# A two-layer encoder kernel on one Trainium2 core: 96 idle bytes at each end of the SBUF pools

## The chip, the cores and the metric

The kernel runs on one core of a Trainium2 chip. A core has TensorE (PE, with its weight loads shown as PEld), VectorE (DVE), ScalarE (ACT), GpSimd (POOL) and SyncE (SP, which here issues every DMA). Operands lie in SBUF, a memory of 128 partitions, and matrix products land in PSUM. The metric is the device time of one execution, in microseconds; lower is better. The figure of a kernel is the median of its runs.

## The reference

The reference is a two-layer encoder on one sequence of 1024 tokens with 1024 features, all in float32. Cut to what matters:

```
for i in range(2):
    shift, scale, gate = split(silu(c) @ ada_w[i] + ada_b[i], 3)
    h = rmsnorm(x, norm_g[i]) * (1 + scale) + shift
    y = diff_attention(h, ...) if i == 0 else latent_attention(h, ...)
    x = x + gate * y
return rmsnorm(x, final_norm_g)
```

Layer 0 is differential attention: 8 heads, two softmaxes of width 64 for each head, the second one subtracted with a learned factor, then a norm for each head, a SiLU gate, and an output projection. Layer 1 is latent attention: queries, keys and values come out of two narrow projections (384 and 256 wide), 64 of the query and key features are rotated by position, 8 heads of width 128, a SiLU gate, an output projection.

## The kernel before, in words

Features or tokens lie on the 128 partitions, and a matrix product is tiled in 128x128 weights times up to 512 moving columns. To reach float32 accuracy every operand is held as two float32r tiles, a high part and a low part, and a product is three matmuls into one PSUM bank (`mm3`, lines 176 to 180):

```
PE.matmul(psum, ah, bh, start=first, stop=False)
PE.matmul(psum, ah, bl, start=False, stop=False)
PE.matmul(psum, al, bh, start=False, stop=last)
```

The first operand is the one loaded as weights, the second one streams. In the names of the profile, `oacc<-woh,o1b3h` is a matmul into `oacc` that streams `woh` over the weights `o1b3h`.

The order of the work is written out by hand: the layer 0 input projection while the modulation weights come in (up to some 180 us), attention of layer 0 with the rest of its projections filled in between the heads (to 676 us), output projection 0, the input projections of layer 1 (lines 1192 to 1514), attention of layer 1, and output projection 1 (`out_proj`, line 1016). Attention lets the PE do, for each block of 128 queries, the scores (L767 in layer 0, L1605 in layer 1), four transposes at a time of the exponentials (L376, streaming the constant tile `ident`), and the products with V (L178 to L180, 256 columns). Fills are steps of a stream of projections (`Stream`, `gen_strips`). SP issues all DMAs in program order.

SBUF is handed out by two stacks of pools. A pool opened with `side="left"` (the default, line 88) lies above the ones that are open on the left; one with `side="right"` lies below those that are open on the right. The two stacks grow toward each other, and a pool that opens where another one has closed waits, tile by tile, for the old tiles' users. On the left lie, from below, `const` (line 98: `ident`, `ones`, `cosT`, `sinT` and small vectors) and `sm` (line 99: small tiles of a few values); above them come and go `p1a`, `a0a`, `pm`, `a0b` (layer 0), `kpp`, `h1`, `p3x`, `p3`, `p4`, `p4v` (projections), `attn1`, `attn1b`, `p6`. On the right the outermost is `wst` (line 126, the weight strips `wraw`, `wh`, `wl`), and below it `H`, `wp0`, `p1b`, `xp`, `OT0`, `pw0`, `u`, `wp1`, `lora`, `pv1`, `OT1`, `pw1`.

A tile takes a multiple of 32 bytes in each partition. The large tiles have 1024, 2048 or 4096 bytes, so all large tiles of one side share their remainder to 128. In the program as built, the first large tile of `const` starts at byte 16512, a multiple of 128. The small tiles of `const` and `sm` then shift what lies above: the lowest large tile of the left pools starts at byte 28064, which is 32 more than a multiple of 128 (and 160 more than a multiple of 256). The right stack ends at byte 229344, and its large tiles, such as `wraw` at byte 206816, lie 96 above a multiple of 128 (224 above a multiple of 256). Between the two stacks at least 576 bytes are free at every time.

A product's two operands can therefore lie on the same side or on opposite ones. Counted over the program's matmuls by the addresses of their two operands: 3849 matmuls of 512 columns have both on one side (2856 right, 993 left); 627 of 512 columns have them on opposite sides (513 stream a left tile over right weights, 114 the reverse), and 18 of 256 columns do. The 1566 products with V of 256 columns are all left with left. 1152 transposes stream `ident`. Of the 627, 300 are in the layer 1 input projections (the first four token blocks of `h1` and the combination tiles `t4` lie on the left, the strips in `wst` on the right), 327 in the two output projections, where `p3` and `p6` hold their late weights on the left and `OT0`, `xp`, `OT1` the attention outputs on the right, or where the pools are the other way round.

Of the kernel before, what the change touches and what calls it, by code (L numbers as in the profile page):

```python
# [11 lines left out]
F32 = mybir.dt.float32  # L12
# [9 lines left out]
P = 128  # L22
# [46 lines left out]
X_CUT = 256  # L69
FIN_LAG = 1  # L70
SKEW = 1
GUARD = 2.0 ** 40
FMAX = 3.4028e38
LAM0 = 0.8 - 0.6 * math.exp(-0.3 * 0)
# [9 lines left out]
def trunk(ctx: ExitStack, tc: tile.TileContext, A, out):  # L84
# [3 lines left out]
    def pool(stack, name, bufs=1, side="left", space=None):  # L88
        kw = dict(name=name, bufs=bufs, reuse_waits="tile")
        if space is not None:  # L90
            kw["space"] = space
            if space == DRAM:
                kw.pop("reuse_waits")
        else:
            kw["side"] = side
        return stack.enter_context(tc.tile_pool(**kw))

    const = pool(ctx, "const")
    sm = pool(ctx, "sm", bufs=4)
    pst = ExitStack()  # L100
    ps = None
    NB = {}
# [20 lines left out]
        return ps.tile(shape or [P, HF], F32, name=name, tag=tag, bufs=NB[tag])  # L123

    dr = pool(ctx, "dr", bufs=1, space=DRAM)
    wst = pool(ctx, "wst", side="right")


# [17 lines left out]
    def part(name):  # L146
        lo, n = VEC[name]
        return vec[:, lo : lo + n]
# [6 lines left out]
    g8 = const.tile([P, 1], F32, name="g8")  # L155
    V.tensor_scalar(g8, part("subln_g"), 0.5 * (1.0 - LAM0) * math.sqrt(P) / GUARD, None, op0=ALU.mult)
    qag, kvg, inv = part("q_a_norm_g"), part("kv_a_norm_g"), part("inv")
# [136 lines left out]
    side = Side()  # L294
# [152 lines left out]
    def gen_mods(load, c2):  # L447

        g, bsh, bsc, a_, b_ = mods[1]
        for j in range(KT):  # L450
            for i, (bias, acc) in enumerate(((bsh, b_), (bsc, a_))):
                mod_dot(load(A["ada_ss1"][j, i]), bias[:, j : j + 1], acc[:, j : j + 1], c2)
                if j == KT - 1 and i == 1:
                    V.scalar_tensor_tensor(out=a_, in0=a_, scalar=1.0, in1=g, op0=ALU.add, op1=ALU.mult)
                yield
        yield from gen_gate(0, load, c2)
# [16 lines left out]
    def h_chunk(l, xn4, k, dst, hp, sub=G, wide=False, act=False, f32=None):  # L473

        _, _, _, a_, b_ = mods[l]
        if wide:
            tr = bank("cb", "trc", [P, D])[:, :HF].rearrange("p (j q) -> p j q", j=4)
        else:
            tr = bank("tr", "trh", [P, 4, P])
        for j in range(len(xn4)):  # L480
            nk = KT // len(xn4[j])
            PE.transpose(tr[:, j, :], xn4[j][k // nk][:, (k % nk) * P : (k % nk + 1) * P], ident)
        n = len(xn4)
        hh, hl = dst
        ak, bk = a_[:, k : k + 1], b_[:, k : k + 1]
        tmp = f32.rearrange("p (j q) -> p j q", j=4) if f32 is not None else hp.tile([P, n, P], F32, name="h32", tag="h32", bufs=2)
        S.activation(hh, tr[:, :n, :], AF.Identity, bias=bk, scale=ak)
        if act:
            S.activation(tmp, tr[:, :n, :], AF.Identity, bias=bk, scale=ak)
        else:  # L490
            V.tensor_scalar(tmp, tr[:, :n, :], ak, bk, op0=ALU.mult, op1=ALU.add)
        return sub.tensor_sub(hl, tmp, f32v(hh)).ins
# [110 lines left out]
    mods_g = gen_mods(lambda src: mod_home[0](src), c2)  # L603
    for k in range(-1, KT + SKEW):
        if k + 1 < KT:
# [18 lines left out]
        if 0 <= k < KT:  # L624
            h_chunk(0, xs0, k, h0[k][0], p1, act=True)
        if k < SKEW:
            continue
        k0, (wh, wl) = k - SKEW, wv0[k - SKEW]
        hh, hl = h0[k0][0]
# [200 lines left out]
    def head_out(o_, o, sq):  # L830


        S.activation(sq, o_, AF.Square, scale=1.0 / GUARD)
        S.mul(o, o_, g8[:, 0:1])

    def subln(o, sq, zz, half, h, dst):
# [7 lines left out]
        def rest():  # L844
# [5 lines left out]
            V.tensor_mul(fin, zz, zz)  # L850
            V.scalar_tensor_tensor(out=w, in0=fin, scalar=P * EPS / GUARD ** 2, in1=pt[:, 0:4], op0=ALU.mult, op1=ALU.add)
            V.scalar_tensor_tensor(out=fin, in0=fin, scalar=FMAX / GUARD ** 2, in1=w, op0=ALU.mult, op1=ALU.is_ge)
            V.tensor_scalar(w, w, 3.0e38, None, op0=ALU.min)
# [983 lines left out]
```

## Time and profile before

| what | value |
|---|---|
| median of 3 runs | 1440.59 us (1439.78 to 1441.86) |
| span of the profiled execution, first to last instruction | 1437.4 us |
| its time beside the span | not given apart; the median lies 3.2 us above the span |
| mean granted TensorE clock in it | 0.995 of full speed |
| matmuls in it | 7388 |

The page of the profile gives the busy time of each engine, the same in 40 slices of the span, the DMA queues, the chain of work that ended last, and the costliest groups of instructions. Matmuls overlap: a 128x512 matmul shows a duration near 390 ns, while the next one starts some 230 ns after it. So the pace of TensorE is read from starts, not from durations. In a timeline row the columns are start, duration, engine, line, operation, output and inputs, shapes and count.

### The profile page before, as it was taken

The numbers are of one execution on the slowest core, as the hardware profiler recorded it, in microseconds if no ns is written. First come the engines' busy times: TensorE is split into PE (matmuls) and PEld (weight loads), VectorE is DVE, ScalarE is ACT, GpSimd is POOL, SyncE is SP. The second block draws the span as 40 slices with busy tenths as digits, with TensorE's granted clock in tenths as the row PEclk, the third lists the DMA queues.
The fourth block names the chain that finished last, engine by engine and source line by source line (L and its number), as shares of the span: only waits on it lengthen the run. The fifth ranks groups of instructions, "written<-read, shape, count | busy, mean of one in ns | idle before, by whom it ended". The sixth has DMA issues, their size and how long they took to land. (4 is left out here: it accounts for less than half of the span.)

```text
span 1437.4 us, 20644 instructions
## 1 busy us (share of the span) xinstructions
PE 1388.9 (97%) x7388; PEld 1159.2 (81%) x7388; DVE 920.2 (64%) x1372; ACT 727.4 (51%) x1287; POOL 611.7 (43%) x483
## 2 busy tenths in 40 slices
PE   5999999999999999998999999999999999999997
PEld 4778788888888887887777877887888888888886
DVE  6657777667777767677435885545666555555355
ACT  5533366656565656566343443335455554545342
POOL 4416064656464646463562334532141331412572
PEclk9999999999999999999999999999999999999999
DMA  9787823233333333337663146398343433336563
GB/s 329 236 247 224 264 67 103 81 105 83 100 87 97 91 93 89 88 96 237 227 201 124 40 132 190 122 296 246 125 128 114 130 98 78 105 97 212 188 234 140
DMA packets 135527, 213.70 MB, mean 149 GB/s; under 512 B 19072, under 2 KB 56064, under 8 KB 135424
## 3 DMA queue, kind: packets, MB, share of 16 engines
q1 hardware_dynamic: 135424, 212.38, 48.6%
q8 instruction: 58, 0.95, 0.3%
q14 instruction: 45, 0.37, 0.1%
HBM read 137.92 MB, written 50.80 MB: 131 GB/s over the span
## 5 line engine op out<-in xcount | busy, mean ns | idle before, releaser
L378 ACT CAST pth<-tr 128x512 fp32r<-128x512 f32 x256 | 150.2, 587 | 282.4 <-PE tr L376 280.8
L393 DVE TENSOR_REDUCE nm<-s 128x1 f32<-128x1024 f32 x192 | 233.9, 1218 | 75.6 <-PE s L767 64.1
L379 DVE TENSOR_TENSOR ptl<-tr,pth 128x512 fp32r<-128x512 f32 x256 | 176.0, 687 | 139.0 <-ACT pth L378 138.4
L224 POOL TENSOR_TENSOR wl<-wraw,wh 128x512 fp32r<-128x512 f32 (+2 forms) x79 | 104.0, 1319 | 204.5 <-ACT wh L223 196.0
L395 ACT ACTIVATE e<-s,nm 128x1024 f32<-128x1024 f32 x128 | 143.5, 1121 | 29.2 <-DVE nm L393 28.7
L376 PE MATMUL tr<-ident,e 128*128 128x128 f32 x1024 | 154.9, 274 | 2.5 <-DVE ptl L379 2.3
L376 PEld LDWEIGHTS tr<-ident,e 128*128 128x128 f32 x1024 | 121.3, 140 | 43.3 <-DVE ptl L379 19.6
L178 PE MATMUL acc<-h0h,wh 128*128 128x512 f32 x360 | 149.9, 416 | 2.1 <-DVE v_hl L356 2.0
L178 PE MATMUL pv<-pth,vt 128*128 128x256 f32 x512 | 147.2, 288 | 0.2 <-DMA vt<-vS 0.2
L179 PE MATMUL pv<-ptl,vt 128*128 128x256 f32 x512 | 145.9, 285 | 0.0
L180 PE MATMUL pv<-pth,vt 128*128 128x256 f32 x512 | 144.6, 282 | 0.0
L180 PE MATMUL acc<-h0h,wl 128*128 128x512 f32 x360 | 142.3, 395 | 0.5 <-POOL wl L224 0.5
L179 PE MATMUL acc<-h0l,wh 128*128 128x512 f32 x360 | 141.4, 393 | 0.0
L1007 POOL TENSOR_TENSOR wol<-wor,woh 128x512 fp32r<-128x512 f32 x64 | 86.3, 1373 | 83.3 <-ACT woh L1006 78.1
L178 PEld LDWEIGHTS pv<-pth,vt 128*128 128x128 f32 x512 | 97.6, 191 | 3.5 <-DMA vt<-vS 0.7
L179 PEld LDWEIGHTS pv<-ptl,vt 128*128 128x128 f32 x512 | 97.7, 191 | 2.6
L180 PEld LDWEIGHTS pv<-pth,vt 128*128 128x128 f32 x512 | 97.7, 191 | 0.1
L320 POOL TENSOR_TENSOR rp_r<-rp_raw,cosT 128x512 f32<-128x512 f32 x38 | 49.8, 1311 | 92.2 <-ACT rp_raw L315 52.1
L325 POOL TENSOR_TENSOR rp_sw<-rp_sw,sinT 128x512 f32<-128x512 f32 x42 | 54.9, 1307 | 76.1 <-DMA rp_sw<-rp_raw 69.6
L767 PE MATMUL s<-ks,qa 128*128 128x512 f32 x256 | 82.1, 402 | 3.6 <-DVE e L775 3.2
L775 DVE SCALAR_TENSOR_TENSOR e<-s,z,e 128x1024 f32<-128x1024 f32 x64 | 82.1, 1283 | 2.1
L767 PE MATMUL s<-ks,qb 128*128 128x512 f32 x256 | 80.9, 395 | 0.0
(590 smaller groups left out, 3340.3 us busy)
## 6 DMA issues: line engine op xcount, KB each, us to landing
ada<-in_ada_ss SPq DMA_DIRECT2D x32, 512.0 KB, 5.9
wraw<-in_w_s SPq DMA_DIRECT2D x64, 256.0 KB, 3.0
vS<-v_hl SPq DMA_DIRECT2D x32, 512.0 KB, 5.8
vt<-vS SPq DMA_DIRECT2D x32, 512.0 KB, 4.2
wor<-in_w_out SPq DMA_DIRECT2D x64, 256.0 KB, 4.2
rp_sw<-rp_raw SPq DMA_DIRECT2D x168, 64.0 KB, 2.0
bc_s<-bc_d SPq DMA_DIRECT2D x34, 256.0 KB, 4.3
oS<-bc_s SPq DMA_DIRECT2D x30, 256.0 KB, 2.5
```

The costliest lines, as they stand in the source:

```text
L178: PE.matmul(psum, ah, bh, start=first, stop=False)
L179: PE.matmul(psum, ah, bl, start=False, stop=False)
L180: PE.matmul(psum, al, bh, start=False, stop=last)
L224: sub = (V if pair_of else G).tensor_sub(l_[:, :n], raw[:, :n], f32v(h_[:, :n]))
L376: PE.transpose(tr[:, j, :], p[:, kt * P : (kt + 1) * P], ident)
L378: mk["S"] = S.copy(pth[kh][:, :, dst], tr).ins
L379: mk["V"] = V.tensor_sub(ptl[kh][:, :, dst], tr, f32v(pth[kh][:, :, dst])).ins
L393: mk["V"] = V.reduce_max(nm, s_ps, axis=AX.X, negate=True).ins
L395: mk["S"] = S.activation(e, s_ps, AF.Exp, bias=nm, scale=1.0, accum_out=zs).ins
L767: PE.matmul(s_ps[:, kc * HF : (kc + 1) * HF], src[:, c, ql], KS[h][kc][:, c, :], start=fst, stop=not fst)
L775: combined.append(V.scalar_tensor_tensor(out=e0, in0=e1, scalar=z1[:, 0:1], in1=e0, op0=ALU.mult, op1=ALU.add).ins)
L1007: in_turn(G.tensor_sub(lo, raw, f32v(hi)))
```

## The change

Two pools are added, each with one tile that nothing reads or writes. `padl` opens on the left above `const` and `sm` and takes 96 bytes; `padr` opens first on the right and takes 96 bytes at the top. Both stay open to the end. Every later left tile moves up by 96 bytes and every right tile down by 96.

```diff
@@ -69,6 +69,8 @@
 SKEW = 1
+PADL = 96 // 4
+PADR = 96 // 4
 GUARD = 2.0 ** 40
@@ -97,6 +99,8 @@
     const = pool(ctx, "const")
     sm = pool(ctx, "sm", bufs=4)
+    padl = pool(ctx, "padl")
+    padl.tile([P, PADL], F32, name="padl")
     pst = ExitStack()
@@ -123,6 +127,8 @@
     dr = pool(ctx, "dr", bufs=1, space=DRAM)
+    padr = pool(ctx, "padr", side="right")
+    padr.tile([P, PADR], F32, name="padr")
     wst = pool(ctx, "wst", side="right")
```

By the addresses above, the left large tiles then start at 28160, a multiple of 512, and the right ones, as `wraw` at 206720, lie 128 above a multiple of 256. No instruction, DMA, wait or size is added or taken away.

## The prediction

> **What bounds the kernel now.** I read the page first: the busy shares, the slices, the chain that ended last.
>
> ```profile
> span 1437.4 us, 20644 instructions
> ...
> PE 1388.9 (97%) x7388; PEld 1159.2 (81%) x7388; DVE 920.2 (64%) x1372; ACT 727.4 (51%) x1287; POOL 611.7 (43%) x483
> ...
> PE   5999999999999999998999999999999999999997
> ...
> PEclk9999999999999999999999999999999999999999
> DMA  9787823233333333337663146398343433336563
> ...
> PE 37%; DVE 2%; DMA 1%; issue 1%; POOL 1%; ACT 0%; SPq 0%; POOLq 0%; ACTq 0%
> ```
>
> TensorE is busy in 97% of the span, in every slice but the first and the last, at full granted clock. The other engines and the DMA carry 5% of the chain between them. So the change can matter in two ways: through the pace of TensorE, or through the little that is not TensorE. No instruction, DMA or wait changes, and with at least 576 bytes free between the stacks both still fit after giving up 192. Shifting every left tile by 96 up and every right tile by 96 down, I compared which left tile lies over which right one: large tiles come in steps of 1024, 2048 or 4096 bytes, and a left and a right tile that overlapped still do, one that did not still does not. So the waits for reused memory stay the same, and all that is left is what an address does to an access.
>
> **The pace of TensorE by sides.** Next I read TensorE's timeline in output projection 1, where matmuls follow one another without a gap and nothing changes but the tiles.
>
> ```profile
> 1376.88 0.39 PE L178 MATMUL oacc<-woh,o1a5h 128*128 128x512 f32 x1
> ...
> 1385.05 0.40 PE L180 MATMUL oacc<-woh,o1a7l 128*128 128x512 f32 x1
> 1385.28 0.40 PE L178 MATMUL oacc<-woh,o1b0h 128*128 128x512 f32 x1
> ...
> 1390.64 0.40 PE L180 MATMUL oacc<-woh,o1b1l 128*128 128x512 f32 x1
> ...
> 1392.96 0.39 PE L178 MATMUL oacc<-woh,o1b2h 128*128 128x512 f32 x1
> ...
> 1393.64 0.39 PE L178 MATMUL oacc<-woh,o1b3h 128*128 128x512 f32 x1
> ...
> 1404.29 0.39 PE L180 MATMUL oacc<-woh,o1b6l 128*128 128x512 f32 x1
> ```
>
> The first stretch (36 matmuls from 1376.88 to 1385.05) streams weights of `p6`, left, over outputs in `OT1`, right: 8.17 us over 35 steps, 233.4 ns each. The second (24 matmuls to 1390.64) streams `pw1`, right, over `p6`, left: 5.36 over 23 steps, 233.0 ns. The third (48 matmuls, 1393.64 to 1404.29) has both operands in `p6`: 10.65 over 47 steps, 226.6 ns. Opposite sides cost 6.6 ns a matmul, 2.9%, and the sign of the offset does not matter: the weights begin 64 bytes further (mod 128) in the first and 64 bytes less in the second. An offset of +64 and one of -64 are the same thing only for a pattern that repeats every 128 bytes, in which 64 is the worst place; then the new offset between the sides, 128, is as good as none. That is my reading; no row has an offset of 128. The same shows elsewhere:
>
> ```profile
> L178 PE MATMUL zacc<-t4h,wh 128*128 128x512 f32 x12 | 4.7, 394 | 0.0
> ...
> L178 PE MATMUL zacc<-t2h,wh 128*128 128x512 f32 x12 | 4.7, 392 | 0.0
> ...
> L178 PE MATMUL zacc<-t1h,wh 128*128 128x512 f32 x12 | 4.7, 389 | 0.0
> ```
>
> Three operands of one product in layer 1's input projection over strips in `wst`, right: `t4` is left and takes 394 ns by duration, `t1` and `t2` are right and take 389 and 392.
>
> **Term 1, the mixed matmuls.** By the addresses 627 matmuls of 512 columns have operands on opposite sides. At the full 6.6 ns they would give 627 x 6.6 = 4.1 us. But same-sided ones do not always run at 226.6: `t1` and `t2` average 390.5, where 389 stands for 226.6 and 394 for 233.4. So the mixed ones should fall by (394 - 390.5)/(394 - 389) = 70% of 6.6, 4.6 ns; 300 of them in the input projections make 1.4 us. In the output projections the runs are long, and a run needs a while to reach the best pace (from 1390.64 to 1392.96 ten steps took 232 ns each after the side changed); I take 5.5 ns for the other 327, 1.8 us. Together **3.2 us**, between 0 and 4.1. Does the end feel it? The stretches in question:
>
> ```profile
> 1358.00:1426.00 68.00, 68.00 (x306) 55.74 (x305) 38.76 (x92) 27.16 (x56) 43.08 (x31) 1.00 0.58 199
> 880.00:945.00 65.00, 63.16 (x275) 50.91 (x274) 35.71 (x51) 23.63 (x42) 36.87 (x27) 1.00 0.54 180
> 740.00:830.00 90.00, 87.82 (x411) 70.55 (x409) 63.62 (x85) 37.21 (x59) 26.66 (x19) 1.00 0.27 88
> ```
>
> Here the first busy number is TensorE's: 68.0 of 68, 63.2 of 65, 87.8 of 90. Nothing else is waited for, so I count the gain in full. If PE came earlier to a tile that a DMA or POOL has not finished, part would go back; the idle 4.0 of 223 us say that this is rare.
>
> [...]
>
> **Term 2, same-sided matmuls and transposes.** Offsets inside a side do not change, so I take 0 for the 3849 same-sided matmuls. In attention they run in short groups between transposes:
>
> ```profile
> 1196.51 1.39 PE s L1605 x6
> 1197.90 0.44 PE tr L376 x4
> 1198.33 0.94 PE s L1605 x4
> ```
>
> Six in 1.39 us are 231.7 ns each, four in 0.94 are 235, so 5 to 8 ns above the best pace. If equal remainders on all sides kept the best pace across groups, up to 3849 x 5.1 = 20 us could go. If the transposes were hurt by `ident` (remainder 0) and `e` (32) becoming equal, 6.6 ns on 1152 of them would cost 7.6 us. Against both:
>
> ```profile
> L376 PE MATMUL tr<-ident,e 128*128 128x128 f32 x1024 | 154.9, 274 | 2.5 <-DVE ptl L379 2.3
> ...
> L482 PE MATMUL trh<-ident,xth x8: 272/272/273, 61.8 to 69.8; 128*128 128x128 f32 x8
> ...
> L847 PEld LDWEIGHTS ssq<-ones,osq x120: 186/192/192, 209.0 to 670.8; 128*128 128x128 f32 x120
> ...
> L1314 PEld LDWEIGHTS cps<-ones,csum x32: 186/192/337, 830.7 to 867.8; 128*128 128x128 f32 x32
> ...
> L824 PEld LDWEIGHTS rb<-sq,ones x8: 186/192/192, 704.5 to 705.3; 128*128 128x128 f32 x8
> ```
>
> A transpose of `e` (32, mean 274 ns) and one of `xth` (right, 96, median 272) take the same, and a weight load takes a median of 192 ns whether its tile lies at 32 (`osq`), 96 (`csum`) or already at 0 (`ones`). Alignment alone buys nothing that these rows show. I take **0**, with -20 and +7.6 as bounds.
>
> **Term 3, the other engines and DMA.**
>
> ```profile
> L325 POOL TENSOR_TENSOR rp_sw<-rp_sw,sinT 128x512 f32<-128x512 f32 x42 | 54.9, 1307 | 76.1 <-DMA rp_sw<-rp_raw 69.6 <-DMA wraw<-in_w_s 4.4 <-ACT rp_raw L317 1.9
> ...
> L223 ACT CAST wh<-wraw 128x512 fp32r<-128x512 f32 x62 | 38.4, 619 | 25.8 <-PE acc L179 14.0 <-issue 3.5 <-DMA wraw<-in_w_s 3.0
> ...
> L492 POOL TENSOR_TENSOR h0l<-h,h0h 128x512 fp32r<-128x512 f32 x14 | 18.2, 1307 | 18.4 <-DVE h L491 10.2 <-ACT h L489 8.0
> ...
> L1331 ACT CAST c_h<-craw 128x512 fp32r<-128x512 f32 x10 | 6.1, 620 | 5.1 <-DVE craw L1323 5.1
> ```
> ```profile
> wraw<-in_w_s SPq DMA_DIRECT2D x64, 256.0 KB, 3.0
> ...
> zraw<-in_w_s SPq DMA_DIRECT2D x12, 256.0 KB, 2.9
> ```
>
> POOL takes 1307 ns with `sinT` (at 0) and without; ACT 619 right to right and 620 right to left; the same strips land in 3.0 us on the right and 2.9 on the left. I take 0, with 0.1 of 3.0 us on DMA's 1% of the chain (14 us) as the bound: 0.5 us either way.
>
> [...]
>
> **The sum.** 1437.4 - 3.2 = 1434.2 us of span. The runs' median lies 3.2 us above the span of the profiled execution, and I carry that over: 1440.6 - 3.2 = **1437.4 us**.
>
> **The rivals.**
>
> 1. Nothing moves: the sides differ by something other than their remainder (their distance, say), or opposite sides stay at 233 at the new offset. For it: no row has an offset of 128. Against it: both signs of 64 cost the same. Then 1440.6, give or take 0.7.
> 2. The whole of TensorE settles: with left, right and constants at remainder 0, a change of side no longer throws it off the best pace. For it: the ten slow steps after 1390.64. Against it: most groups in attention are cut by transposes, and those stay. At half of the 20 us and the 3.2, 1427; at a quarter, 1432.
> 3. Slower: the pattern repeats every 256 bytes, not 128, and 128 is its worst place, where the left (0 mod 256) and the right (128) now stand. A second 6.6 ns on the 627 mixed matmuls gives 1440.6 + 4.1 = 1444.7. It decides where `oacc<-woh,o1a5h` to `o1a7l` step by more than 233.4 ns, and turns the total past 1443.5 from 4.6 ns more. Against it: in a 256-byte pattern +64 and -64 need not cost the same, yet they do.
>
> **How the numbers follow.** Forecast 0.52, rival 1 0.18, rival 2 0.13, rival 3 0.17. A measurement of this kernel can tell about 0.2%, 2.9 us, from no change: below 1437.7 is faster, above 1443.5 slower. The forecast's own range is 1436.0 to 1438.8, and 0.31 of its 0.52 lies below 1437.7; with rival 2 that is 0.44 faster. The rest of it and rival 1 make 0.39 same, rival 3 0.17 slower. The range for 8 in 10 goes from 1430 (a third of the way into rival 2) to 1443, leaving out most of rival 3 and the far half of rival 2.
>
> **What would show it.** After the change the timeline of output projection 1 should step by 226.6 to 228 ns from `o1a5h` to `o1b7l` whatever the side, and `zacc<-t4h` should read 389 to 391. `acc`, `s` and `tr` in attention should keep their paces, `PEld` its 192, ACT its 620, and the two `in_w_s` loads should stay within 0.1 us. If `o1a5h` still steps by 233, the remainder is not the cause; if it steps by more, rival 3 holds; if six scores take less than 1.37 us, rival 2 does.

## The result, and the profile after

| | before | after |
|---|---|---|
| median of 12 runs each | 1441.49 us (1438.29 to 1443.68) | 1439.87 us (1436.52 to 1443.70) |
| ratio of the times | | 0.9992, 95% interval 0.9981 to 1.0003 |
| span of the profiled execution | 1437.4 us | 1436.9 us |

The interval contains 1: no change that this measurement can tell. The forecast was 1437.4 us, that is 0.9978, just outside the interval; the measured time lies within the stated range of 1430 to 1443 us. The page of the changed kernel hardly differs:

```profile
span 1436.9 us, 20644 instructions
...
PE 1388.8 (97%) x7388; PEld 1158.8 (81%) x7388; DVE 917.5 (64%) x1372; ACT 728.7 (51%) x1287; POOL 610.6 (42%) x483
...
PEclk9999999999999999999999999999999999999999
...
q1 hardware_dynamic: 135424, 212.38, 47.1%
...
PE 38%; DVE 2%; issue 1%; POOL 1%; ACT 1%; POOLq 0%; ACTq 0%
```

TensorE is busy for 1388.8 us against 1388.9. Only the share of the DMA queue is visibly smaller: 47.1% here. The page of the kernel before has

```profile
q1 hardware_dynamic: 135424, 212.38, 48.6%
```

for the same bytes. The prediction said where to look, output projection 1. TensorE's timeline there, in the changed kernel (start, duration, engine, line, operation):

```profile
1376.13 0.40 PE L184 MATMUL oacc<-woh,o1a5h 128*128 128x512 f32 x1
...
1384.30 0.39 PE L186 MATMUL oacc<-woh,o1a7l 128*128 128x512 f32 x1
1384.53 0.40 PE L184 MATMUL oacc<-woh,o1b0h 128*128 128x512 f32 x1
...
1389.89 0.39 PE L186 MATMUL oacc<-woh,o1b1l 128*128 128x512 f32 x1
...
1392.86 0.39 PE L184 MATMUL oacc<-woh,o1b3h 128*128 128x512 f32 x1
...
1403.51 0.40 PE L186 MATMUL oacc<-woh,o1b6l 128*128 128x512 f32 x1
```

The first stretch takes 8.17 us for 35 steps, the second 5.36 for 23, the third 10.65 for 47: 233.4, 233.0 and 226.6 ns, to the digit what they took before. The addresses did act: single steps of the first stretch were 233 or 234 ns before, and now alternate between 229 or 230 and 237 or 238. Their mean did not move.

Summed over the whole trace, taking every start-to-start step of a 512-column matmul under 250 ns and counting what lies above 226.7 ns, the matmuls with operands on opposite sides lost 3.7 us before and 3.8 after; the same-sided ones 11.6 before and 13.2 after. The change bought nothing where gain was forecast, and cost 1.6 us where nothing was.

### The profile page after: what moved, and what is told of

Read it like the earlier page. It is cut to its first block, busy times and chain, and to the rows that moved or that the text cites. A ratio compares the mean times of both kernels' runs of the same rounds, so it can differ in the third digit from the quotient of the medians.

```text
span 1436.9 us, 20644 instructions
## 1 busy us (share of the span) xinstructions
PE 1388.8 (97%) x7388; PEld 1158.8 (81%) x7388; DVE 917.5 (64%) x1372; ACT 728.7 (51%) x1287; POOL 610.6 (42%) x483
## 3 DMA queue, kind: packets, MB, share of 16 engines
q1 hardware_dynamic: 135424, 212.38, 47.1%
```

## The experiments

Theory A: the pace is set by the offset between two operands, as forecast, but with another period and other values. Theory B: it is set by the side or the distance. Theory C: by the absolute remainder to 128. Each ratio below is to the kernel before, run beside it on the same chip. A step is the time from one matmul's start to the next one's. "Mixed" means matmuls with operands on opposite sides.

**Offsets alone.** All products of the encoder are replaced by

```
for k in range(8):
    for i in range(4):
        c = slice(wo // 4 + i * P, wo // 4 + (i + 1) * P)
        PE.matmul(accs[i], wh[:, c], mh[:, m], start=k == 0, stop=False)
        PE.matmul(accs[i], wh[:, c], ml[:, m], start=False, stop=False)
        PE.matmul(accs[i], wl[:, c], mh[:, m], start=False, stop=k == 7)
```

> This kernel leaves out the whole encoder: it runs only matmuls on constant tiles, in the pattern of the output projection (three matmuls a product, four 128-column weight slices in turn, 512 moving columns, 96 in a row for each case), and writes zeros. The moving tiles start at a multiple of 512 bytes. Cases n0w to n480w: weights on the same side, starting 0 to 480 bytes (steps of 32) above a multiple of 512. b32w to b96w: moving and weights both shifted by the same 32, 64, 96 bytes. f0w, f64w, f128w, f256w, f448w: weights on the other side of SBUF, some 200,000 bytes away, at these offsets. Theory A (the offset of the two operands within 512 bytes sets the pace): n0w, b32w, b64w, b96w and f0w step by 226.7 ns; n128w, n448w, f128w and f448w by 233.3; far and near agree at each offset. Theory B (the distance or the side sets it): all n and b cases 226.7, all f cases 233.3. Theory C (the absolute remainder to 128 sets it): n0w and n128w 226.7, b32w to b96w slower.

TensorE's timeline, the first row of some cases; each case has 96 matmuls, so the difference to the first row of the next case, divided by 96, is the step:

```profile
49.53 0.40 PE L112 MATMUL n64w<-mh,nh 128*128 128x512 f32 x1
...
71.93 0.39 PE L112 MATMUL n96w<-mh,nh 128*128 128x512 f32 x1
...
94.41 0.39 PE L112 MATMUL n128w<-mh,nh 128*128 128x512 f32 x1
...
116.71 0.39 PE L112 MATMUL n160w<-mh,nh 128*128 128x512 f32 x1
...
139.12 0.40 PE L112 MATMUL n192w<-mh,nh 128*128 128x512 f32 x1
...
161.10 0.40 PE L112 MATMUL n224w<-mh,nh 128*128 128x512 f32 x1
...
183.50 0.39 PE L112 MATMUL n256w<-mh,nh 128*128 128x512 f32 x1
...
205.26 0.39 PE L112 MATMUL n288w<-mh,nh 128*128 128x512 f32 x1
...
405.22 0.39 PE L112 MATMUL b96w<-mh,nh 128*128 128x512 f32 x1
...
427.01 0.39 PE L112 MATMUL f0w<-mh,fh 128*128 128x512 f32 x1
...
448.81 0.40 PE L112 MATMUL f64w<-mh,fh 128*128 128x512 f32 x1
...
471.21 0.39 PE L112 MATMUL f128w<-mh,fh 128*128 128x512 f32 x1
...
493.53 0.39 PE L112 MATMUL f256w<-mh,fh 128*128 128x512 f32 x1
```

An offset of 64 gives 233.3 ns, 96 gives 234.2, 128 gives 232.3, 160 gives 233.4, 192 gives 229.0, 224 gives 233.3, 256 gives 226.7, and from 256 to 480 the same numbers come again in the same order. Far tiles do as near ones: f0w 227.1 (226.7 once settled), f64w 233.3, f128w 232.5. Both operands shifted by 96 (b96w) run at 227.0, so an unaligned address costs at most 0.3 ns by itself. B and C fall; A holds with a period of **256 bytes**, in which 0 is free, 128 costs 5.6 ns and no other multiple of 32 is free (229.0 to 234.2 ns).

**Equal remainders, unaligned.**

```diff
+PADL = 64 // 4
+    padl = pool(ctx, "padl")
+    padl.tile([P, PADL], F32, name="padl")
```

> Left tiles 64 bytes up, right tiles unmoved: all large tiles of both sides 480 above a multiple of 512, so equal remainders, none aligned to 128. Theory A (offset of the operands within 512 bytes): the stretches with opposite sides (o1a5h to o1a7l, o1b0h to o1b1l) step by 226.7 instead of 233.3 ns; 627 such matmuls give 3 to 4 us, time 1437 to 1438 beside 1441 of the kernel before. Theory B (side or distance): they keep 233.3, time as before, 1441. Theory C (absolute alignment): as before or like the changed kernel.

Measured: 1440.03 us, ratio 1.000 (0.9989 to 1.001). The pace did what A says, mixed steps of 227.1 ns on average and 0.3 us of loss left of 3.7, and the time did not follow.

**Equal remainders, aligned, and 256 apart.** Both as in the change, with other sizes:

```diff
-PADR = 96 // 4
+PADR = 480 // 4
```

> Left tiles 96 up as in the change, right tiles 480 down: all large tiles at multiples of 512, equal and aligned. Theory A: the same paces and the same time as with equal unaligned remainders, 1437 to 1438. Theory B: 233.3 ns on opposite sides, 1441. Theory C: faster here than with the equal unaligned remainders.

```diff
-PADR = 96 // 4
+PADR = 224 // 4
```

> Left tiles 96 up, right tiles 224 down: the sides are 256 bytes apart within 512, all tiles at multiples of 256. Theory A with a period of 512: opposite sides step by more than 226.7 ns (some 229 to 234), time 1439 to 1442; with a period of 256: 226.7 and 1437 to 1438. Theory B: 233.3 and 1441.

Measured: 1437.83 us, ratio 0.9981 (0.9972 to 0.9990), and 1437.67 us, ratio 0.9979 (0.9970 to 0.9988). Output projection 1 with the sides 256 apart:

```profile
1373.97 0.39 PE L184 MATMUL oacc<-woh,o1a5h 128*128 128x512 f32 x1
...
1381.90 0.39 PE L186 MATMUL oacc<-woh,o1a7l 128*128 128x512 f32 x1
1382.13 0.39 PE L184 MATMUL oacc<-woh,o1b0h 128*128 128x512 f32 x1
...
1387.34 0.39 PE L186 MATMUL oacc<-woh,o1b1l 128*128 128x512 f32 x1
```

7.93 us over 35 steps and 5.21 over 23: 226.6 and 226.5 ns. That is the forecast's pace, and within 0.3 us the forecast's time, at an offset of 256 instead of 128. The period of 256 holds in the kernel too. That these two gained and the unaligned one did not is not explained by the pace.

**Own weights or the next ones.**

> This kernel leaves out the encoder: 96 matmuls in a row for each case, 512 moving columns, new 128-column weights for every matmul, constant tiles, output zeros. While one matmul streams, the weights of the next are being loaded, so the conflict may be between a matmul's moving tile and its own weights, or between it and the next matmul's. own128w alternates two matmuls so that each matmul's own pair is 128 bytes apart (within 256) while the moving tile and the next weights are equal; next128w the reverse; both128w has both apart. If the next weights matter: own128w 226.7 ns a step, next128w and both128w some 232.4. If the own pair matters: own128w 232.4, next128w 226.7. The same with 64. s4w to s24w: offsets of 4, 8, 16 and 24 bytes; if the memory is read in units of 32 bytes, 4 and 8 may cost as little as 0; a fine conflict pattern gives 228 to 234.

TensorE's timeline, one merged row for each case (start, time of 96 matmuls):

```profile
27.92 21.92 PE L103 MATMUL eqw<-m,w 128*128 128x512 f32 x96
49.68 22.40 PE L103 MATMUL own64w<-m,w 128*128 128x512 f32 x96
71.92 22.40 PE L103 MATMUL next64w<-m,w 128*128 128x512 f32 x96
94.15 22.56 PE L103 MATMUL both64w<-m,w 128*128 128x512 f32 x96
116.55 22.25 PE L103 MATMUL own128w<-m,w 128*128 128x512 f32 x96
138.64 22.08 PE L103 MATMUL next128w<-m,w 128*128 128x512 f32 x96
160.56 22.46 PE L103 MATMUL both128w<-m,w 128*128 128x512 f32 x96
182.86 22.46 PE L103 MATMUL s4w<-m,w 128*128 128x512 f32 x96
```

By the starts, own128w steps by 230.1 ns, next128w by 228.3, both128w by 232.3; own64w and next64w by 231.7 and 231.6 (there +64 and -64 alternate, so 128 is the cleaner case). Neither simple answer holds: a matmul is slowed by an offset to its own weights and by one to the weights of the next. So a same-sided matmul followed by one whose weights lie on the other side can pay as well, and in attention the fills and scores alternate between the sides. Offsets of 4, 8, 16 and 24 bytes cost too: 232.3, 230.7, 233.3 and 230.0; there is no free unit of 32 bytes.

**Transfers alone.**

> This kernel leaves out the encoder and writes zeros: it only moves tiles of 128 rows of 2048 bytes, eight stores to HBM in a row from SBUF addresses 0, 32, 64, 96, 128, 192 and 256 bytes above a multiple of 512, and loads from HBM to such addresses, each series twice. If the transfers feel the SBUF address, the stores (and perhaps the loads) at 32 and 96, or at all but multiples of 128 or 256, take some per cent more time a packet than those at 0; if they don't, all are alike within 1%.

SP's queue, first series of stores (start, time to issue eight). The DMA queue takes 99.9% of the 16 engines' span at a mean of 380 GB/s; eight stores of 256 KB in 5.45 us are 385 GB/s, so the issue runs at the pace of the transfers, and a store lands a median of 2.8 to 3.1 us after its issue:

```profile
1.94 4.26 SPq L100 DMA_DIRECT2D st0a<-z  x8
6.25 5.34 SPq L100 DMA_DIRECT2D st32a<-z  x8
11.63 5.45 SPq L100 DMA_DIRECT2D st64a<-z  x8
17.13 5.46 SPq L100 DMA_DIRECT2D st96a<-z  x8
22.64 5.45 SPq L100 DMA_DIRECT2D st128a<-z  x8
28.13 5.44 SPq L100 DMA_DIRECT2D st192a<-z  x8
33.61 5.06 SPq L100 DMA_DIRECT2D st256a<-z  x8
```

Stores from 256 take 5.06 us, from 64 to 192 5.44 to 5.46, 8% more (the first row, 4.26, is the start of the series: that it is short because transfers were not yet queued is the author's reading; st0b, in the second series, took 4.94). For the loads the median time to landing was 5.0 to 5.4 us in the second series, 5.2 at 256, 5.1 at 32 and 5.4 from 64 to 192; no order by alignment is settled.

**Equal remainders of 64, and of 128 with ident.**

```diff
-PADL = 96 // 4
-PADR = 96 // 4
+PADL = 32 // 4
+PADR = 32 // 4
```

> Left tiles 32 bytes up, right tiles 32 down: both sides at 64 above a multiple of 128, their remainders to 512 equal (448). TensorE's stretches on opposite sides should step by 226.7 ns as with the equal remainders of 480 and of 0. If the share of the DMA queue (48.6% before, 47.1 to 47.4 with the tiles at multiples of 128) and the 2 to 3 us at the start hang on multiples of 128, this kernel has 48.5% and a time near 1440; if multiples of 64 are enough, 47.3% and 1437.5 to 1438.5.

```diff
-PADL = 96 // 4
-PADR = 96 // 4
+PADL = 224 // 4
+PADR = 352 // 4
```

> Left tiles 224 bytes up, right tiles 352 down: both sides and the constant tiles (ident, ones, cosT, sinT) 128 above a multiple of 512, so every large tile has the same remainder. Opposite sides should step by 226.7 ns; if the transposes or the groups between them feel the remainder of ident, the scores in attention should fall from 230.7 ns (left, 512 columns) towards 228 and up to 5 us be gained: 1433 to 1435. If not, the time is that of the kernel with all at multiples of 512, 1437.8, when 128 is enough for the DMA, and up to 1440 when it needs 256.

Measured: 1439.84 us, ratio 0.9987 (0.9974 to 1.0000), and 1439.50 us, ratio 0.9989 (0.9975 to 1.0002), both inconclusive as times. Mixed losses were 0.3 and 0.4 us. The DMA queue's share was 47.8% with 64 and 47.0% with 128. 512-column steps with both operands on the left take 230.0 ns on average with `ident` at the same remainder, 230.7 in the kernel with all tiles at multiples of 512 (`ident` 128 off), and 229.8 with equal remainders of 64 (`ident` 64 off). That refutes the 5 us: the remainder of the constant tile is not what keeps the attention above its best pace.

**The same programs again.** Three kernels were profiled a second time, unchanged.

> The kernel before, profiled once more, to see what differs between two executions of one program. Theory D (the pace by addresses is fixed, while the stretches in which matmuls step by 427 instead of 227 ns fall differently in every execution): the mixed matmuls again have 3.7 us above 226.7 ns a step (3.6 to 3.8) and the others 11.6 (11.2 to 12.0), but the number of 427 ns steps is not 21 again: anything from 10 to 50, and the start of attention 0 moves by 1 to 3 us. Against it: the number is 19 to 23, and the 2 us that the changed kernel gained at the start are its addresses' doing.

> The changed kernel, profiled once more. Theory D: mixed matmuls again 3.8 us above the best pace, the others 13.2 (12.8 to 13.6), so 1.6 more than before in both executions; the number of 427 ns steps is not 14 again; the start of attention 0 differs from 138.7 us by up to 3. Against it: it is 138.7 within 0.5.

> The kernel with the sides 256 bytes apart, profiled once more. Mixed matmuls 0.4 us above the best pace and the others 11.1 (10.8 to 11.5) as in the first execution; 427 ns steps 20 to 50, most of them again between 785 and 900 us, because TensorE arrives earlier there and waits longer, which is no accident of one execution; the DMA queue's share 47.3%, give or take 0.2.

| | before | before again | after | after again | 256 apart | 256 apart again |
|---|---|---|---|---|---|---|
| span, us | 1437.4 | 1441.2 | 1436.9 | 1435.3 | 1434.5 | 1436.6 |
| mixed, us above 226.7 ns | 3.7 | 3.7 | 3.8 | 3.8 | 0.4 | 0.3 |
| other 512-column, us above | 11.6 | 11.7 | 13.2 | 13.4 | 11.1 | 11.3 |
| steps of 427 ns | 21 | 36 | 14 | 16 | 36 | 26 |
| of these at 785 to 900 us | 5 | 21 | 7 | 8 | 20 | 10 |
| first matmul to attention 0, us | 140.8 | 139.5 | 138.7 | 138.5 | 138.7 | 140.4 |
| share of the DMA queue, % | 48.6 | 48.0 | 47.1 | 47.3 | 47.3 | 47.0 |

The rows of pace repeat within 0.2 us, so 1.6 us more for the other matmuls after the change is no accident of one execution. The 427 ns steps do not repeat. Against theory D, the changed kernel's start repeated, 138.7 and 138.5; the kernel with the sides 256 apart moved by 1.7. For that kernel only 10 of 26 such steps fell at 785 to 900, not most, and the execution with fewer of them took 2.1 us longer. Such steps look like this in the timeline of the kernel before:

```profile
856.95 1.24 PE L1314 MATMUL cps<-ones,csum 128*128 128x1 f32 x8 [2.10 <-DVE csum L1309]
858.05 0.77 PE L178 MATMUL acc<-h1h,wh 128*128 128x512 f32 x1
858.62 0.63 PE L179 MATMUL acc<-h1l,wh 128*128 128x512 f32 x1
859.05 0.63 PE L180 MATMUL acc<-h1h,wl 128*128 128x512 f32 x1
859.48 0.63 PE L178 MATMUL acc<-h1h,wh 128*128 128x512 f32 x1
```

TensorE waits 2.10 us for `csum`; shortly after, matmuls take 0.63 us and start 427 ns apart, 1.9 times 226.7. The granted clock (the column after the engine's busy time) shows the same in the stages 826 to 866 and 866 to 900 us, first of the kernel before, then of its second execution:

```profile
826.00:866.00 40.00, 36.73 (x164) 0.96 0.41 120
866.00:900.00 34.00, 32.16 (x143) 1.00 0.65 208
```
```profile
826.00:866.00 40.00, 36.76 (x158) 0.91 0.39 119
866.00:900.00 34.00, 31.84 (x135) 0.95 0.64 200
```

One program, two executions: 0.96 and 1.00 against 0.91 and 0.95, with spans 3.8 us apart. The same wait has different sequels: 1.17 us at about 830 us was followed by no step of 427 ns in the first execution and by seven in the second, 2.1 us at about 857 by five and by eight. In the changed kernel's two executions 1.2 us at 830 and 2.1 us at 893 had no such step after them, and in the second execution of the kernel before 2.1 us at 894 had six. Of the 21 slow steps in the kernel before, 16 fall where the granted clock is 0.50: from 52.1 to 58.8 us, after a wait of 2.11 us at 51.2, and from 857.7 to 860.9; from 826.0 to 857.5 and from 861.1 to 866.0 it is 1.00. In the changed kernel it is 0.50 from 857.1 to 860.3. Four slow steps before 21 us fall where it reads 1.00. Waits of 1.2 to 2.1 us were followed by slow steps here, and waits as long by none. What decides between the two is not shown; no run here moved one wait alone.

**Keeping TensorE busy.** On top of the kernel with the sides 256 apart:

```diff
             pt = bank("tr", "cps", [P, 4, P])
+            if half == 0:
+                busy = h1[0][0][0]
+                for _ in range(6):
+                    PE.matmul(pt, busy[:, :P], t3(busy), start=True, stop=True)
             for j in range(4):
```

> The sides 256 bytes apart, and besides twelve matmuls whose results nobody reads: six before the first cps product of each of the two narrow projections, where TensorE waits 1.5 and 2.3 us for a sum of squares. (The compiler's order of a few neighbours moves too: one cps product by six matmuls, some DMAs of c_h.) If the 427 ns steps after these waits give back what the better pace gains, they vanish between 826 and 865 us (13 of them, 2.6 us), and the time falls from 1437.7 to 1435 to 1436.5; if the end of this stage hangs on POOL and its wl strips anyway, TensorE only waits longer at 890 and the time stays at 1437.7, give or take 1; if the added matmuls come late, 1439.

Measured: 1431.58 us, ratio 0.9934 (0.9914 to 0.9954), below everything that was expected. Its timeline and its two stages:

```profile
826.72 1.52 PE L1322 MATMUL cps<-h_0h 128*128 128x512 f32 x6
828.27 1.05 PE L1324 MATMUL cps<-ones,csum 128*128 128x1 f32 x8
```
```profile
826.00:866.00 40.00, 39.97 (x192) 1.00 0.47 138
866.00:900.00 34.00, 32.67 (x144) 1.00 0.64 208
```

The wait for `csum` is covered, the granted clock is 1.00 in both stages, and of the 427 ns steps from 826 to 900 us one is left, of 20 and 5 in the two executions of the kernel without the added matmuls. From the first `cps` product to the first score of layer 1 the kernel needs 140.2 us, against 145.2 and 143.0, although it runs twelve matmuls more. At 200 ns each, the missing slow steps make 3.8 of the first difference and 0.8 of the second. The five runs lie between 1430.2 and 1432.1, the nine of the kernel before beside them between 1436.0 and 1444.3. Not separated: the compiler also moved one `cps` product and some DMAs, and some of the 6.1 us between 1437.67 and 1431.58 may be theirs. This version is 9.1 us faster than the kernel before beside it.

## Why the prediction was right or wrong, point by point

- **What bounds the kernel: right.** The gains and losses that the runs could place were those of TensorE's pace or its waits.
- **The pace of TensorE by sides: the offset is the cause, the period was wrong.** The step that failed is "the sign of the offset does not matter", read from two stretches of one place; from it came the period of 128 bytes, and that an offset of 128 "is as good as none". The sign does matter: alone, +64 (n64w) runs at 233.3 ns and -64 (n192w) at 229.0. The period is 256 bytes, and 128 costs 5.6 ns. The kernel before already showed the difference in a stretch that the prediction does not quote, 24 matmuls of `h0h` and `h0l`, right, over `wq`, left:

```profile
100.65 0.39 PE L178 MATMUL acc<-h0h,wq 128*128 128x512 f32 x1
...
105.91 0.39 PE L180 MATMUL acc<-h0h,wq 128*128 128x512 f32 x1
```

  That is 5.26 us over 23 steps, 228.7 ns, at -64. The stretch that was quoted for -64 stepped by 233 all the same, and did so again in the second execution; one and the same offset has more than one steady pattern. Why it did stays open. It follows a stretch of +64 without a gap and may have kept its step; but n192w too follows a case of 233 without a gap, and settles at 229.
- **Term 1: wrong for this change, right in size at another offset.** Forecast 3.2 us for 627 mixed matmuls. At 128, where the change puts them, their loss fell by nothing. With the sides 0 or 256 apart it fell by 3.3 to 3.4 us in five kernels. The time followed less surely: by their medians these five were 0.4, 2.6, 2.8, 1.4 and 1.8 us faster than the kernel before beside them, and only 2.6 and 2.8 are clear of the noise. So that the end feels the gain in full, as the sum counts it, is not shown.
- **Term 2: wrong by 1.6 us.** Same-sided matmuls were taken at 0, since "Offsets inside a side do not change". But a matmul also meets the next matmul's weights (next128w steps by 228.3 ns against 226.7), and between fills and scores these change sides. Sorted by that, the traces place half of the 1.6 us: same-sided matmuls followed by weights of the other side lost 2.8 us before and 3.6 after, those followed by weights of their own side 8.7 and 9.6, and both rose in attention of layer 0. Why the latter rose stays open; with equal remainders the same-sided loss also differed, from 9.6 to 11.5 us in the five kernels named under Term 1. The transposes stayed at a mean of 274 ns, as forecast. The bounds of -20 and +7.6 held.
- **Term 3: a small effect in the queue, its worth open.** The queue's share fell by about 1 point (48.0 to 48.6 before and with the equal unaligned remainders, 47.0 to 47.8 with the tiles at multiples of 64 or more). The store of `xfull` to `x1S` fell from 4.0 and 3.6 us to 3.2 and 3.3, but took 3.7 with all tiles at 128. Alone, eight stores took 7% less time from 256 than from 64 to 192 (5.06 us against 5.44 to 5.46). The stores do not explain the queue's share: it was as low as anywhere, 47.0%, with all tiles at 128, and stores from 128 took as long as from 64. That this made the start of the changed kernel 1 to 2 us shorter, or kept the unaligned kernel from gaining, is not shown: from the first matmul to attention 0 the unaligned kernel took 141.9 us, but the one with all tiles at 128 took 141.8 and the one at 64 138.4.
- **The sum.** Instead of -3.2 stand 0.1 for Term 1 and 1.6 for Term 2; the span nevertheless fell by 0.5 in the first pair of profiles, in which the changed kernel had seven 427 ns steps less and a start 2.1 us shorter. Such things vary by up to some 3 us between executions of one program (21 and 36 such steps in the kernel before, 3.0 us at 200 ns each; 1.7 us at the start with the sides 256 apart), and the prediction had no term for them. That the measured 1439.87 us lies within 1430 to 1443 is luck of a wide range and not the forecast's doing: of the mechanism that was to lower the time, nothing arrived.
- **The rivals.** What came is the second half of rival 1: opposite sides stay at 233 at the new offset, but because the offset matters and 128 is a bad one, not because it does not matter. The line "If `o1a5h` still steps by 233, the remainder is not the cause" would have led to the wrong answer. Rival 3 had the period right and the price wrong: 128 costs 5.6 ns where 64 cost 6.6. Rival 2 is refuted by the kernel with equal remainders everywhere: 1439.5 us, not 1427 to 1432.

## What to carry to other kernels

Where TensorE sets the time, let the tiles that stream and the tiles that are loaded as weights have the same remainder to 256 bytes (226.7 ns a step here); a multiple of 128 is not enough for that (232.3 ns at an offset of 128), and equal remainders do it without any alignment (227.0 with both operands shifted by 96). Here that is worth some 3 us of TensorE's pace in 1440, and in three of five kernels only part of it showed in the time. Before building on a pattern in a profile, find the same case in two places that do not follow each other. And look for waits of TensorE that are followed by slow matmuls: what they cost includes these, and filling such a wait with idle work may save them (one 427 ns step was left here, of 20 and 5), though it does not shorten the wait. Length alone does not tell which waits: one of 1.7 us at about 676 us had no slow matmul after it in any of the eleven profiled executions of the encoder.

## What was not expected of the hardware

- The pace of a matmul depends on its operands' relative address in steps as small as 4 bytes (232.3 ns) and with a period of 256 bytes; distance does not matter (at an offset of 64, 233.3 ns from near by and from some 200,000 bytes away; at 256, 226.7 and 226.8). No other engine works on the tiles of that run once they are filled, and an offset of 64 costs 6.6 ns all the same. That TensorE's own two reads, of the stream and of the weights, disturb each other is the author's reading; no run here shows the reads themselves.
- Nine runs of the kernel before spread over 8 us, and five of the kernel whose two waits were filled over 2. That the 427 ns steps are that spread is only argued: of the two executions of the kernel with the sides 256 apart, the one with ten such steps less took longer.
